# Splitting the first row loads of a top-2 gating kernel further

## The chip, the cores and the metric

The kernel runs on one core of one Trainium2 chip. The metric is device time in microseconds (us), lower is better; the time given is the median of several executions. A profile of one execution is recorded besides; its span (first to last instruction) is a little shorter than the device time.

## The reference

Each of 16 x 1024 tokens has a row `x` of 512 float32 values and 8 router logits. The softmax of the logits gives 8 probabilities; the two largest are kept and scaled to a sum of 1, and the row of `x` is written out twice, once multiplied by each of the two weights, the smaller weight first.

```python
batch, seq, hidden, n_experts, k = 16, 1024, 512, 8, 2

def reference(x, router_logits, k):
    logits_max = np.max(router_logits, axis=-1, keepdims=True)
    probs = np.exp(router_logits - logits_max)
    probs = probs / np.sum(probs, axis=-1, keepdims=True)
    topk_indices = np.argsort(probs, axis=-1)[..., -k:]
    topk_probs = np.take_along_axis(probs, topk_indices, axis=-1)
    topk_probs = topk_probs / np.sum(topk_probs, axis=-1, keepdims=True)
    x_expanded = x[:, :, np.newaxis, :].repeat(k, axis=2)
    return (x_expanded * topk_probs[..., np.newaxis]).astype(np.float32)
```

So 33.5 MB of `x` and 0.5 MB of logits are read from HBM, and 67.1 MB are written to it. There is no matrix product.

## The kernel before

The 16384 tokens are laid over 128 partitions, 128 tokens per partition, in two batches of 65 and 63 tokens per partition. A token's row is 2 KB. All loads of `x` go to one buffer `xs` of 65 tokens per partition, which the second batch fills again. A load of n tokens moves, for each of the 128 partitions, one run of n x 2 KB that is contiguous in HBM: a load of 2 tokens is 128 rows of 4 KB.

```python
GROUPS = [65, 63]

LOADS = [[2, 2, 4, 8, 16, 16, 17], [2, 2, 4, 8, 16, 16, 15]]
...
    L = 16
    ...
    logits = wpool.tile([P, M, E], F32)
    xs = wpool.tile([P, max(GROUPS), D], F32)
    osp = wpool.tile([P, L, 2, D], F32)

    def over(r, n, G):
        a = 2 * r - G
        return xs[:, a : a + 2 * n, :].rearrange("p (r k) d -> p r k d", k=2)

    h = L // 2
    e = 2
    m0 = 0
    for g, G in enumerate(GROUPS):
        r = 0
        for n in LOADS[g]:
            nc.sync.dma_start(xs[:, r : r + n, :], x_v[g][:, r : r + n, :])
            r += n
            if g == 0 and r == L:
                nc.sync.dma_start(logits[:, :G], rl_v[0])
                nc.sync.dma_start(logits[:, G:], rl_v[1])
                WA = top2_weights(nc, wpool, logits, M, E)
        assert r == G
        begin = [(0, e, osp[:, :e]), (e, L - e, osp[:, e:])] if g == 0 else [(0, L, osp)]
        plan = begin + [
            (L, L, over(L, L, 2 * L)),
            (2 * L, h, osp[:, :h]),
            (2 * L + h, h, osp[:, h:]),
        ]
        plan += [(r, n, over(r, n, G)) for r, n in ((48, 8), (56, 4), (60, G - 60))]
        for r, n, og in plan:
            nc.vector.tensor_tensor(
                og,
                xs[:, r : r + n, :].unsqueeze(2).to_broadcast([P, n, 2, D]),
                WA[:, m0 + r : m0 + r + n, :].unsqueeze(3).to_broadcast([P, n, 2, D]),
                op=ALU.mult,
            )

            queue = nc.scalar if n == e else nc.sync
            queue.dma_start(o_v[g][:, r : r + n], og)
        m0 += G
```

The logits of all tokens are loaded once, after the first 16 tokens per partition of `x`. `top2_weights` (lines 13 to 44) finds the two largest logits by 12 VectorE operations in maxima and minima, takes their difference and makes both weights by two sigmoids on ScalarE.

The products (line 125) are made on VectorE, eight of them in the first batch and seven in the second. Their result goes to `osp`, a buffer of 16 tokens, or over rows of `xs` that are no longer needed (`over`). Each is followed by its store (line 133). All loads (line 109) and all stores but one are issued by SyncE, in the order of the program; only the first store, of 2 tokens, is issued by ScalarE. Tile, the layer that the kernel is written in, adds the waits on semaphores: a product waits for its rows and weights, a store for its product, a load of the second batch for the stores that still read the place it fills.

Of the kernel before, what the change touches and what calls it, by code (L numbers as in the profile page):

```python
# [1 line left out]

# [4 lines left out]

F32 = mybir.dt.float32
ALU = mybir.AluOpType
ACTF = mybir.ActivationFunctionType  # L10
P = 128


def top2_weights(nc, pool, logits, M, E):

    hi, lo, n = None, None, E  # L20
    while n > 1:
        n //= 2
        if hi is None:
            a, b = logits[:, :, 0:n], logits[:, :, n : 2 * n]
            nhi = pool.tile([P, M, n], F32, tag=f"hi{n}")
            nlo = b
            nc.vector.tensor_tensor(nhi, a, b, op=ALU.max)  # L27
            nc.vector.tensor_tensor(nlo, a, b, op=ALU.min)  # L28
        else:
            a, b = hi[:, :, 0:n], hi[:, :, n : 2 * n]  # L30
            nhi = pool.tile([P, M, n], F32, tag=f"hi{n}")
            nlo = pool.tile([P, M, n], F32, tag=f"lo{n}")
            tmp = pool.tile([P, M, n], F32, tag=f"tmp{n}")
            nc.vector.tensor_tensor(tmp, lo[:, :, 0:n], lo[:, :, n : 2 * n], op=ALU.max)  # L34
            nc.vector.tensor_tensor(nlo, a, b, op=ALU.min)  # L35
            nc.vector.tensor_tensor(nlo, nlo, tmp, op=ALU.max)  # L36
            nc.vector.tensor_tensor(nhi, a, b, op=ALU.max)  # L37
        hi, lo = nhi, nlo
    dlt = pool.tile([P, M], F32, tag="dlt")
    nc.vector.tensor_tensor(dlt, hi[:, :, 0], lo[:, :, 0], op=ALU.subtract)  # L40
    WA = pool.tile([P, M, 2], F32, tag="WA")
    nc.scalar.activation(WA[:, :, 0], dlt, ACTF.Sigmoid, scale=-1.0)  # L42
    nc.scalar.activation(WA[:, :, 1], dlt, ACTF.Sigmoid, scale=1.0)  # L43
    return WA

GROUPS = [65, 63]

LOADS = [[2, 2, 4, 8, 16, 16, 17], [2, 2, 4, 8, 16, 16, 15]]


@with_exitstack
def kernel(
    ctx: ExitStack,
    tc: tile.TileContext,
    x: bass.AP,
    router_logits: bass.AP,
    k: bass.AP,  # L60
    out: bass.AP,
):
    nc = tc.nc
    B, S, D = x.shape
    E = router_logits.shape[-1]
    N = B * S
    assert int(k) == 2 and E == 8 and N == P * sum(GROUPS)
    M = N // P

    L = 16  # L70
    x_v, o_v, rl_v = [], [], []
    t0 = 0
    for n in GROUPS:
        t1 = t0 + P * n
        x_v.append(
            x.rearrange("b s d -> (b s) d")[t0:t1].rearrange("(p m) d -> p m d", p=P)
        )
        o_v.append(
            out.rearrange("b s k d -> (b s) k d")[t0:t1].rearrange(
                "(p m) k d -> p m k d", p=P  # L80
            )
        )
        rl_v.append(
            router_logits.rearrange("b s e -> (b s) e")[t0:t1].rearrange(
                "(p m) e -> p m e", p=P
            )
        )
        t0 = t1

    wpool = ctx.enter_context(tc.tile_pool(name="wpool", bufs=1))  # L90
# [46 lines that stand above are left out]
# [1 line left out]
_INS = ['x', 'router_logits', 'k']  # L138
_OUTS = [((16, 1024, 2, 512), 'float32')]

_NUMBERS = {'k': 2}


# [26 lines left out]
```

## Time and profile before

| | |
|---|---|
| device time, median of 3 | 240.41 us (240.33 to 240.43) |
| span of the profiled execution | 238.7 us |
| VectorE busy | 142.5 us (60%) |
| ScalarE busy | 1.8 us (1%) |
| DMA packets, bytes | 4464, 101.19 MB |
| first issue of a load on SyncE | 0.73 us |
| logits landed, first VectorE operation | 14.4 us, 14.48 us |
| first product | 18.95 us |
| last product starts, last store issued | 211.65 us, 215.03 us |

How to read it. The profile divides the span into 40 equal slices and gives for each the busy share of an engine in tenths, for the DMA the mean of the core's 16 DMA engines. The list of queues says how much of 16 engines' span the packets of a queue filled. The chain of waits goes back from the last instruction, at each step to what released it. In lists of waits, `SPq` is SyncE's queue, which issues the transfers; an issue is short, and the transfer itself lands later. A DMA packet is here one row of a partition; a DMA ends on each engine with a packet of 4 bytes that signals its completion.

### The profile page before, as it was taken

What the parts mean: (1) busy time and instruction counts of PE and PEld (TensorE: products, weight loads), DVE (VectorE), ACT (ScalarE), POOL (GpSimd) and SP (SyncE); (2) the same over time, 40 slices, a digit from 0 to 9 for tenths busy, and PEclk for the clock granted to TensorE, in tenths of its full rate; (3) what the DMA queues carried; (4) which work ended last, traced back from release to release, by engine and by line L of the source; (5) the groups of instructions that cost most, each with busy time, mean ns of one, the idle gap of its engine ahead of it and who ended that gap; (6) DMA issues with size and microseconds to landing.
All of it is one profiled execution on the core that took longest, in us unless ns stands there. A gap on an engine that the chain in (4) does not pass through costs nothing.

```text
span 238.7 us, 128 instructions
## 1 busy us (share of the span) xinstructions
DVE 142.5 (60%) x26; ACT 1.8 (1%) x3; POOL 0.2 (0%) x4
## 2 busy tenths in 40 slices
DVE  0058999990299699910000699999106999990000
ACT  2000000000000000000000000000000000000000
POOL 0000000000000000000000000000000000000000
DMA  7999998999998999999999999998999989999997
GB/s 253 442 448 439 419 464 375 434 461 461 395 461 351 439 439 439 439 439 406 428 426 439 458 417 412 459 529 373 472 406 406 472 351 439 439 439 439 439 398 305
DMA packets 4464, 101.19 MB, mean 424 GB/s; under 512 B 496, under 2 KB 624, under 8 KB 1264
## 3 DMA queue, kind: packets, MB, share of 16 engines
q1 hardware_dynamic: 4320, 100.14, 97.9%
q10 hardware_dynamic: 144, 1.05, 1.0%
HBM read 34.08 MB, written 67.11 MB: 424 GB/s over the span
## 4 chain that ended last, share of the span: by engine, by line
DMA 41%; DVE 41%; issue 5%; SPq 2%; ACT 0%; DVEq 0%
DVE xs L125 22%; DVE osp L125 17%; DMA out_dram<-osp 13%; DMA out_dram<-xs 12%; DMA xs<-in_x_dram 11%; DMA logits<-in_router_logits_dram 5%; SPq L109 2%; DVE nhi L27 0%; DVE logits L28 0%; SPq L113 0%; DVE nlo L36 0%; DVE nhi L37 0%; DVE nlo L35 0%; DVE tmp L34 0%; SPq L133 0%
## 5 line engine op out<-in xcount | busy, mean ns | idle before, releaser
L125 DVE TENSOR_TENSOR osp<-xs,WA 128x8192 f32<-128x8192 f32 (+3 forms) x7 | 69.1, 9908 | 55.7 <-DMA xs<-in_x_dram 31.3
L125 DVE TENSOR_TENSOR xs<-xs,WA 128x16384 f32<-128x16384 f32 (+4 forms) x8 | 69.5, 8692 | 2.3 <-DMA out_dram<-xs 2.1
L27 DVE TENSOR_TENSOR nhi<-logits 128x512 f32<-128x512 f32 x1 | 0.7, 691 | 14.5 <-DMA logits<-in_router_logits_dram 14.5
L42 ACT ACT_TABLE_LOAD x1 | 1.3, 1283 | 0.7 <-PEq L151 0.7
L28 DVE TENSOR_TENSOR logits<-logits 128x512 f32<-128x512 f32 x1 | 0.7, 691 | 0.0
L37 DVE TENSOR_TENSOR nhi<-nhi 128x256 f32<-128x256 f32 (+1 forms) x2 | 0.7, 352 | 0.0
L35 DVE TENSOR_TENSOR nlo<-nhi 128x256 f32<-128x256 f32 (+1 forms) x2 | 0.7, 352 | 0.0
L36 DVE TENSOR_TENSOR nlo<-nlo,tmp 128x256 f32<-128x256 f32 (+1 forms) x2 | 0.7, 351 | 0.0
L42 ACT ACTIVATE WA<-dlt 128x128 f32<-128x128 f32 x1 | 0.3, 315 | 16.4 <-DVE dlt L40 16.4
L34 DVE TENSOR_TENSOR tmp<-logits 128x256 f32<-128x256 f32 x1 | 0.4, 418 | 0.0
L40 DVE TENSOR_TENSOR dlt<-nhi,nlo 128x128 f32<-128x128 f32 x1 | 0.3, 291 | 0.0
L43 ACT ACTIVATE WA<-dlt 128x128 f32<-128x128 f32 x1 | 0.3, 299 | 0.0
L34 DVE TENSOR_TENSOR tmp<-nlo 128x128 f32<-128x128 f32 x1 | 0.3, 285 | 0.0
L151 POOL MEMSET const-bfloat16-1.0<- 128x1 bf16 x1 | 0.1, 102 | 0.0
L151 POOL MEMSET const-uint8-127<- 128x1 uint8 x1 | 0.1, 102 | 0.0
L151 POOL MEMSET const-float32-1.0<- 128x1 f32 x1 | 0.1, 99 | 0.0
L151 POOL MEMSET const-float32-0.0<- 128x1 f32 x1 | 0.1, 98 | 0.2 <-issue 0.2
## 6 DMA issues: line engine op xcount, KB each, us to landing
xs<-in_x_dram SPq DMA_DIRECT2D x4, 4096.0 KB, 31.2
out_dram<-osp SPq DMA_DIRECT2D x4, 4096.0 KB, 20.7
out_dram<-xs SPq DMA_DIRECT2D x2, 4096.0 KB, 21.2
out_dram<-osp SPq DMA_DIRECT2D x1, 7168.0 KB, 27.7
xs<-in_x_dram SPq DMA_DIRECT2D x1, 4352.0 KB, 41.4
xs<-in_x_dram SPq DMA_DIRECT2D x2, 2048.0 KB, 19.1
out_dram<-xs SPq DMA_DIRECT2D x2, 2048.0 KB, 21.6
xs<-in_x_dram SPq DMA_DIRECT2D x1, 3840.0 KB, 38.2
```

Of the source, the lines that this page charges most:

```text
L27: nc.vector.tensor_tensor(nhi, a, b, op=ALU.max)
L28: nc.vector.tensor_tensor(nlo, a, b, op=ALU.min)
L34: nc.vector.tensor_tensor(tmp, lo[:, :, 0:n], lo[:, :, n : 2 * n], op=ALU.max)
L35: nc.vector.tensor_tensor(nlo, a, b, op=ALU.min)
L36: nc.vector.tensor_tensor(nlo, nlo, tmp, op=ALU.max)
L37: nc.vector.tensor_tensor(nhi, a, b, op=ALU.max)
L40: nc.vector.tensor_tensor(dlt, hi[:, :, 0], lo[:, :, 0], op=ALU.subtract)
L42: nc.scalar.activation(WA[:, :, 0], dlt, ACTF.Sigmoid, scale=-1.0)
L43: nc.scalar.activation(WA[:, :, 1], dlt, ACTF.Sigmoid, scale=1.0)
L109: nc.sync.dma_start(xs[:, r : r + n, :], x_v[g][:, r : r + n, :])
L125: nc.vector.tensor_tensor(og, xs[:, r : r + n, :].unsqueeze(2).to_broadcast([P, n, 2, D]), WA[:, m0 + r : m0 + r + n, :].unsqueeze(3).to_b ...
L151: nc = _bacc.Bacc("TRN2", target_bir_lowering=False, num_devices=1)
```

## The change

The first load of the first batch, of two tokens per partition, is divided into two loads of one token each, and nothing else is touched. The first loads of that batch then have rows of 2, 2, 4, 8 and 16 KB where they had 4, 4, 8 and 16; the second of 4 KB and the later ones stay as they were. The first sixteen tokens are still loaded ahead of the logits. It is meant to bring the first data on the way with smaller pieces and let the queue get going earlier. (The 4 KB rows of the second batch's first two loads are left.)

```diff
-LOADS = [[2, 2, 4, 8, 16, 16, 17], [2, 2, 4, 8, 16, 16, 15]]
+LOADS = [[1, 1, 2, 4, 8, 16, 16, 17], [2, 2, 4, 8, 16, 16, 15]]
```

## The prediction

> **What bounds the kernel now.** I read the page first, then the windows of the start and of the end, then the chain of waits, the waits of the issuing queue, and last the trace's records of single DMA packets. On the page the two rows of slices belong together: the upper is VectorE, the lower the mean busy share of the 16 DMA engines, in tenths.
>
> ```profile
> DVE 142.5 (60%) x26; ACT 1.8 (1%) x3; POOL 0.2 (0%) x4
> DVE  0058999990299699910000699999106999990000
> DMA  7999998999998999999999999998999989999997
> q1 hardware_dynamic: 4320, 100.14, 97.9%
> HBM read 34.08 MB, written 67.11 MB: 424 GB/s over the span
> ```
>
> VectorE is idle for whole slices and the DMA engines never are: only the first and the last slice are below 8. The SyncE queue's packets alone fill 97.9% of 16 engines. The next view gives busy times in stretches; the last two columns are the DMA share (it can pass 1, since a packet is counted where it starts) and GB/s.
>
> ```profile
> 0.00:1.60 1.60, 0.00 (x0) 0.87 (x1) 0.20 (x4) 1.00 0.00 0
> 1.60:2.60 1.00, 0.00 (x0) 0.41 (x1) 0.00 (x0) 1.00 0.80 106
> 2.60:4.80 2.20, 0.00 (x0) 0.00 (x0) 0.00 (x0) 1.00 1.01 395
> 4.80:14.40 9.60, 0.00 (x0) 0.00 (x0) 0.00 (x0) 1.00 1.06 445
> 14.40:60.00 45.60, 38.34 (x14) 0.52 (x2) 0.00 (x0) 1.00 1.02 434
> 180.00:237.00 57.00, 33.77 (x5) 0.00 (x0) 0.00 (x0) 1.00 1.00 432
> 237.00:238.70 1.70, 0.00 (x0) 0.00 (x0) 0.00 (x0) 1.00 0.02 7
> ```
>
> So data moves from about 1.7 us to 237.5, where the last packet ends (it is counted where it started, before 237), without a gap. What isn't full rate is 1.6 us of nothing, one poor microsecond at 106 GB/s, and some 1.2 us after the last byte. The span is therefore: time to the first packet, a loss while the first reads get going, the work of all packets, and the end. Only these four can change it.
>
> The chain of waits names VectorE for 41% of the span, and this must not mislead. Three pieces of it, start and length in us:
>
> ```profile
> 3.25 11.12 DMA logits<-in_router_logits_dram
> 53.53 29.77 DMA out_dram<-xs
> 150.68 30.43 DMA out_dram<-osp
> ```
>
> A store issued at 53.53 lands at 83.30, and one issued at 150.68 at 181.11. A 16-row store is 8 MB, some 19.5 us at 430 GB/s, so each stood about 10 us behind other transfers in the queue. I did this for the other stores as well (issue time from the timeline, landing of the transfer ahead of it from the semaphore events): 36.27 against 47.0, 72.77 against 83.3, 167.94 against 181.1, 198.46 against about 210. **The work waiting ahead of each is about 10 us everywhere**, so VectorE can be late by far more than a microsecond before a DMA engine runs dry.
>
> The first product also waits for the logits (14.5 us in the list of waits), not for the first rows. The issuing queue's own waits on loads are small:
>
> ```profile
> DVE nhi L27 <- DMA logits<-in_router_logits_dram: 14.5, 1, 14.5
> SPq L109 <- DMA xs<-in_x_dram: 1.1, 2, 0.9
> 0.73 1.81 SPq L109 DMA_DIRECT2D xs<-in_x_dram  x4
> 2.58 0.63 SPq L113 DMA_DIRECT2D logits<-in_router_logits_dram  x1
> ```
>
> Four issues in 1.81 us are one every 0.47 us (0.38 to 0.43 us of work and 0.05 between).
>
> **What the Trainium skill says.** All four places are on the page "DMA: Bandwidth & Descriptors".
> - "Latency and other measured facts" gives about 600 ns to the first byte for transfers issued from SyncE. The trace agrees: the first issue ends at 1.11 us and the first packet starts at 1.735, 0.62 us later.
> - "Where 436 GB/s comes from" puts the ceiling of the 16 ports at 435 GB/s, and expects some 358 for traffic with HBM. The trace has 432 to 434 GB/s over long stretches: the 435 holds here, the 358 doesn't.
> - "Why small descriptors are slow (HBM only)" names a fixed cost per packet. The trace agrees, and I take its size from the trace, below.
> - "Rules for kernel authors" asks for at least 1 MiB per DMA. The first loads here are 512 KB, and packets behind them start every 155.5 ns on each engine with no gap, because later DMAs are queued by then; the rule doesn't bite.
>
> **The change part by part.** For the first batch of 65 rows per partition, the first 4 rows come as 1, 1 and 2 in place of 2 and 2. The loads of 4, 8, 16, 16 and 17 rows stay, the logits still follow row 16, and the second batch is untouched. VectorE and ScalarE do the same work.
>
> *Removed:* 128 packets of 4096 bytes (one load of 128 partition rows of 4 KB). *Added:* 256 packets of 2048 bytes (two loads of 2 KB rows) and one more set of 16 completion packets of 4 bytes. Per DMA engine: 8 packets of 4 KB go, 16 of 2 KB and one completion come.
>
> Cost of a packet, from the records of single packets, as the distance between successive starts on one engine while reads alone run:
>
> ```
> bytes    ns from start to start
>  2016     78.7
>  2080     81.3   (the logits)
>  4096    155.5
>  8192    305.9
> ```
>
> From 4096 to 8192 is 150.4 ns for 4096 bytes, 0.0367 ns a byte; 4096 bytes then cost 150.4, and the 5.1 left over is the fixed part. It gives 81.5 for the 2080 bytes of the logits (81.3 seen), so it carries down to this size. 2048 bytes lie between the two logits sizes: 80.0 ns. A completion packet takes 6 ns before the next data packet starts.
> - removed: 8 x 155.5 = 1244 ns
> - added: 16 x 80.0 + 6 = 1286 ns
> - **difference: +42 ns** on every engine, and on the path, since the engines are never idle afterwards.
>
> *The added issue:* 0.47 us on SyncE. Loads and logits behind it are issued 0.47 us later (logits at 3.05 in place of 2.58). This lies beside transfers: with the first sixteen rows issued the queue holds 4 MB in both kernels, over 9 us of work. At the front I checked for a gap: a 2 KB-row load is 0.64 us of transfer, longer than the 0.47 us between issues. The second load's packets can start about 0.62 us after its issue ends at 1.59, so at 2.2; the first is not through before about 3.0. No gap. The two issues that wait for an early load (the second 16-row load, until 4.37, and the 17-row load, until 5.62) may move by up to about 1 us; the queue then has work until about 14 us.
>
> *The start itself:* the first issue stays at 0.73, so the first packet should stay at 1.735. What follows is the one term that I can't work out. Before, the 16 engines finish the first load (8 packets each, 1.24 us at the steady pace) between 3.56 and 4.00 us, 3.80 in the mean, where 1.735 + 1.24 would be 2.98: **a loss of 0.82 us**. The first packet of the engines takes 186 to 993 ns, 588 in the mean. I take this as a latency, paid once whatever the size of the packets: change 0.
>
> Sum: 240.41 + 0.04 + 0 = **240.45 us**.
>
> **The rivals.**
> 1. *The starting loss goes with the bytes of the first packet.* That must be what the change hopes for: first rows half as long, first data half as late. Halving 588 ns saves 0.29 us, and with the 0.04 the time would be 240.16. For it: the first packets are slow, not only late. Against it: several are through in 186 ns with the same 4096 bytes, so bytes don't set their time, and what a first packet saves the next may pay.
> 2. *The starting loss goes with the number of packets.* Up to 2.6 us, 26 packets had started, 1.6 per engine. If so many are slow whatever they carry, the half-size ones bring half the bytes, and 1.6 x (155.5 - 80.0) = 0.12 us are lost: 240.57. For it: starts are sparse up to 2.6 and regular afterwards. Against it: some engines have two or three through by then.
> 3. *VectorE becomes the limit*, since the logits land later. In the ring order their packets stand behind the same 4 MB, so they land about 0.04 us later; even 0.47 us is small against the 10 us of margin. Change 0.
> 4. *A reordered queue.* One more DMA shifts which completion semaphore each later DMA shares with an earlier one. A store that must wait for a transfer still running would cost microseconds. Against it: the sharers are seven or eight transfers back, and the reloads that wait (15.7 us in the waits of the queue) wait for stores that read the same buffer, which stays so. About 1 in 50.
>
> **Range and chances.** The known part is +0.04. Rivals 1 and 2 put the ends at 240.16 and 240.57; three runs of the kernel before spread by 0.10 us, which I add in part on both sides. So 240.2 to 240.7 at 8 in 10. Two per cent would be 4.8 us; the whole start up to 2.6 us is less than that, so a gain of 2% is out of reach, and a loss of 2% needs rival 4. Chances: 0.003 faster, 0.99 same, 0.007 slower.
>
> **What would show it.** In the profile after: 4608 packets in place of 4464 (128 data and 16 completions more), five loads in the first group of issues, first packet near 1.7 us, logits issued near 3.05 and landed near 14.4, VectorE's first work near 14.5, the last packet's end near 237.5. If the window from 1.6 to 2.6 us moves clearly more than 106 GB/s and the logits land near 14.1, rival 1 is right; if they land at 14.5 or later, rival 2. A dip of the DMA slices in mid-span would be rival 4, and would make the prediction wrong.

## The result and the profile after

The changed kernel takes **242.55 us** (242.34 to 243.09, 4 runs) against 240.42 for the kernel before: ratio 1.0091, 95% interval 1.0074 to 1.0109. The prediction said 240.45, at most 240.7. The change costs 2.1 us, fifty times the 0.04 us that the packets were to cost. (The profiled execution, from which the traces below come, is the longest of the four, 243.09 us; that of the kernel before took 240.51.)

The page of the changed kernel, the lines that answer to those of before:

```profile
DVE 142.5 (59%) x26; ACT 1.8 (1%) x3; POOL 0.2 (0%) x4
DVE  0018999992099889920000599999105999990000
DMA  6999999999999999999999999999999999999994
DMA packets 4608, 101.19 MB, mean 419 GB/s; under 512 B 512, under 2 KB 640, under 8 KB 1408
q1 hardware_dynamic: 4464, 100.14, 97.0%
```

The work is the same to the packet: 4608 packets, as foreseen, and the same 142.5 us of VectorE. The mean rate fell from 424 to 419 GB/s. The row of slices hides where, for it is a mean over 16 engines in slices of 6 us. The windows of the same profile show it (the last two columns are DMA share and GB/s):

```profile
1.60:2.60 1.00, 0.00 (x0) 0.41 (x1) 0.00 (x0) 1.00 0.62 172
2.60:4.80 2.20, 0.00 (x0) 0.00 (x0) 0.00 (x0) 1.00 0.92 290
4.80:14.40 9.60, 0.00 (x0) 0.00 (x0) 0.00 (x0) 1.00 0.97 374
14.40:30.00 15.60, 12.38 (x13) 0.51 (x2) 0.00 (x0) 1.00 1.04 445
237.00:238.00 1.00, 0.00 (x0) 0.00 (x0) 0.00 (x0) 1.00 0.67 283
238.00:239.00 1.00, 0.00 (x0) 0.00 (x0) 0.00 (x0) 1.00 0.20 86
239.00:240.00 1.00, 0.00 (x0) 0.00 (x0) 0.00 (x0) 1.00 0.12 49
```

The start is better than before (172 in place of 106 GB/s), and then it turns: 290 where 395 stood, 374 where 445 stood. Note also the share beside the rate: 0.97 busy at 374 GB/s means packets that are counted as running and wait. Others are not even running: by the packet records, 12.8 packets are under way at once from 3.5 to 4.8 us, where the kernel before has 16.4, so three or four of the 16 engines stand without one. From 14.4 us on the rate is as before. The last three lines are the bill: at 237 us the kernel before had next to nothing left to move (7 GB/s from there to its end), and here the rate falls from 283 to 49 GB/s over three more microseconds, as one engine after the other is done.

The chain of waits has the logits landing 2.5 us later (3.53 + 13.34 = 16.87 in place of 14.38), and the timeline of SyncE's queue has what I had not foreseen, issues that take long:

```profile
3.53 13.34 DMA logits<-in_router_logits_dram
0.73 2.28 SPq L109 DMA_DIRECT2D xs<-in_x_dram  x5
3.06 0.43 SPq L113 DMA_DIRECT2D logits<-in_router_logits_dram  x1
3.53 1.11 SPq L114 DMA_DIRECT2D logits<-in_router_logits_dram  x1
4.68 3.60 SPq L109 DMA_DIRECT2D xs<-in_x_dram  x3
```

The second issue of logits takes 1.11 us, where it took 0.44, and the first of the three loads behind it 1.36.

The trace has sixteen semaphore events for each DMA, one from each DMA engine, so it gives a landing per engine. First and last of the 16, in us:

```
                       before             after
first load             3.91 to 4.37       2.83 to 3.44
second load            5.17 to 5.62       3.62 to 4.07
third load             7.65 to 8.11       5.10 to 7.93
logits, second half   13.91 to 14.38     14.81 to 16.87
last store           237.31 to 237.85    237.65 to 240.50
```

(The third load is the one of 4 tokens before and of 2 after.) The engines of the kernel before stay about half a microsecond apart in these rows. In the changed kernel they part during the third load, and the distance is not made up in the remaining 230 us: the first engine ends 0.3 us later than before, the last 2.65. A load has 128 packets and 16 completion events, so 8 packets to an engine, and a late engine is not seen to get help. The waits don't end with the third load either: of the 128 packets of the 4-token load behind it, which start between 4.8 and 9.8 us, 48 take longer than the 309 ns of the kernel before, up to 1600.

### The profile page after: what moved, and what is told of

Read it like the earlier page. It is cut to its first block, busy times and chain, and to the rows that moved or that the text cites. A ratio compares the mean times of both kernels' runs of the same rounds, so it can differ in the third digit from the quotient of the medians.

```text
span 241.3 us, 131 instructions
## 1 busy us (share of the span) xinstructions
DVE 142.5 (59%) x26; ACT 1.8 (1%) x3; POOL 0.2 (0%) x4
## 2 busy tenths in 40 slices
DMA packets 4608, 101.19 MB, mean 419 GB/s; under 512 B 512, under 2 KB 640, under 8 KB 1408
## 4 chain that ended last, share of the span: by engine, by line
DMA 42%; DVE 40%; issue 5%; SPq 2%; ACT 0%; DVEq 0%
DVE xs L125 22%; DVE osp L125 17%; DMA out_dram<-osp 13%; DMA out_dram<-xs 12%; DMA xs<-in_x_dram 12%; DMA logits<-in_router_logits_dram 6%; SPq L109 2%; DVE nhi L27 0%; DVE logits L28 0%; DVE nlo L36 0%; DVE nhi L37 0%; DVE nlo L35 0%; DVE tmp L34 0%; SPq L113 0%; SPq L133 0%
```

## The experiments

All change only how the first batch is loaded. "Time" is the median; "logits" is the landing of the second half of the logits, first and last engine, in the one execution that was profiled. The ratio is to the kernel before on the same chip.

```
first batch                     time us   ratio (95% interval)      logits
before  2 2 4 8 16 16 17        240.42                              13.91 to 14.38
after   1 1 2 4 8 16 16 17      242.55    1.0091 (1.0074, 1.0109)   14.81 to 16.87
set 1   1 3 4 8 16 16 17        240.58    0.9979 (0.9957, 1.0000)   13.74 to 14.82
        2 1 1 4 8 16 16 17      240.97    1.0007 (0.9995, 1.0019)   14.69 to 15.24
        2 2 4 8 8 8 16 17       240.57    0.9996 (0.9977, 1.0015)   13.87 to 14.25
        1 1 6 8 16 16 17        243.10    1.0092 (1.0060, 1.0124)   14.12 to 17.36
set 2   8 1 1 6 16 16 17        240.62    0.9978 (0.9957, 0.9998)   13.91 to 14.41
        1 1 1 1 4 8 16 16 17    242.42    1.0060 (1.0037, 1.0082)   14.17 to 15.82
        2 in two halves, 2 4 .. 243.03    1.0082 (1.0051, 1.0113)   15.08 to 16.96
        1 15 16 16 17           240.77    0.9985 (0.9963, 1.0007)   13.68 to 14.39
set 3   16 16 16 17             240.86    1.0012 (1.0005, 1.0019)   13.68 to 14.62
        1 x8, 8 16 16 17        241.72    1.0048 (1.0034, 1.0061)   14.74 to 15.65
        4 1 1 10 16 16 17       240.59    1.0001 (0.9992, 1.0009)   13.89 to 14.63
        after, 2nd on ScalarE   240.57    1.0000 (0.9992, 1.0009)   13.94 to 14.55
```

(In sets 1 and 2, 22 of 68 executions of the kernel before took 241.7 to 242.6 us, and so did 4 of 20 of the kernel 2 2 4 8 8 8; none of these was profiled and the reason stays open, and as they shift the ratios of these sets a little, the medians are the better guide.)

The last engine's landing of the logits and the time of the same execution go together: in twelve of the fourteen rows they lie 225.6 to 226.5 us apart, 226.1 before and 226.2 after the change. So what the change costs has happened to the slowest engine by the time the logits land. The two other rows are 1 3 4 (227.1) and 16 16 16 17 (227.4). Their profiled executions took 241.93 and 242.03 us, the longest of 12 and of 22, and one engine fell back further after the logits; they don't speak for the medians.

**Set 1: is it the rows or the number of DMAs?** The changed kernel has both 2 KB rows and one DMA more.

```diff
-LOADS = [[2, 2, 4, 8, 16, 16, 17], ...
+LOADS = [[1, 3, 4, 8, 16, 16, 17], ...
```

> First batch loaded as 1, 3, 4, 8, 16, 16, 17: one 2 KB-row load in front, no added DMA. Rows theory (2 KB rows in front make the engines stall once the 4 KB and 8 KB rows follow, each engine keeps its own delay to the end): some of the 2.1 us, 241.0 to 242.5. Count theory (one DMA more in the first issues backs up SyncE's descriptor work, seen as issues of 1.1 and 1.4 us in place of 0.43, and starves engines): as before, 240.3 to 240.6. Chance theory (every kernel with another start draws other stalls): anywhere from 239.8 to 243.

Measured: 240.58, not to be told from the kernel before. The range of the rows theory (241.0 and more) is missed. In the profiled execution, the longest, fifteen engines stay together (they land the 4-token load between 7.48 and 7.82 us) and one is 0.76 us behind them (8.58).

```diff
+LOADS = [[2, 1, 1, 4, 8, 16, 16, 17], ...
```

> First batch loaded as 2, 1, 1, 4, 8, 16, 16, 17: as many DMAs and 2 KB rows as the change has, but the 4 KB-row load stays first. Rows theory, where only the first packets matter: about 240.45 (0.04 us of packet cost). Count theory: 242 to 243, with issues of the logits or of the load after them over 1 us. Chance theory: 239.8 to 243.

Measured: 240.97, issues of 0.43 us. Between the theories: a small loss, most of it not at the 2 KB rows but behind them. The first sixteen packets of the 4-row load that follows show it, in ns, in order of start; the same load in the kernel before beside it:

```
2 1 1 4:  1267 1413 531 519 1446 1342 1088 994 1126 618 928 319 319 613 309 309
before:    309  309 309 309  309  309  309 309  309 309 309 309 309 309 309 309
```

Most engines wait at the start of the next load, by different times; later packets of that load average 14 ns more than 309.

```diff
+LOADS = [[2, 2, 4, 8, 8, 8, 16, 17], ...
```

> First batch loaded as 2, 2, 4, 8, 8, 8, 16, 17: one DMA more, none of 2 KB rows, and the added one stands after the logits, when 4 MB are queued. Rows theory: 240.4 to 240.6. Count theory: slower by 1 to 2.5 us if it is the number of descriptors in the queue that matters, as before if it is their number before the logits. Spread of the 16 engines at the landing of the logits: 0.5 us by the rows theory, over 1.5 us by the count theory.

Measured: 240.57 in the median, spread of the engines 0.4 us. One DMA more behind the logits costs nothing.

```diff
+LOADS = [[1, 1, 6, 8, 16, 16, 17], ...
```

> First batch loaded as 1, 1, 6, 8, 16, 16, 17: the change's two 2 KB-row loads with no added DMA. Rows theory: about as the changed kernel, 242 to 243. Count theory: 240.3 to 240.6. Chance theory: 239.8 to 243.

Measured: 243.10 without any added DMA, and the long issue is back at the same place: the seventh issue, here the first of the 16-row loads, takes 1.38 us of the 3.12 below. The timeline of SyncE's queue and two windows of this kernel:

```profile
3.04 0.43 SPq L114 DMA_DIRECT2D logits<-in_router_logits_dram  x1
3.51 3.12 SPq L109 DMA_DIRECT2D xs<-in_x_dram  x3
```

```profile
2.60:3.50 0.90, 0.00 (x0) 0.00 (x0) 0.00 (x0) 1.00 0.98 366
3.50:4.80 1.30, 0.00 (x0) 0.00 (x0) 0.00 (x0) 1.00 0.96 358
4.80:8.00 3.20, 0.00 (x0) 0.00 (x0) 0.00 (x0) 1.00 1.00 370
```

The kernel before in the last two of these windows:

```profile
3.50:4.80 1.30, 0.00 (x0) 0.00 (x0) 0.00 (x0) 1.00 1.02 419
4.80:8.00 3.20, 0.00 (x0) 0.00 (x0) 0.00 (x0) 1.00 1.08 458
```

The count theory falls; two 2 KB-row loads in front are enough. The chance theory is weakened, not gone: the four executions here lie between 242.97 and 243.38, the twelve of 2 1 1 4 between 240.49 and 241.23, but the kernel before varies by 2 us with one and the same start. Between 3.5 and 4.0 us only 12 packets of the 6-row load start, so some of the 16 engines stand without any packet at all. That pointed to descriptors: the Trainium skill's page "DMA: Bandwidth & Descriptors", section "SWDGE vs HWDGE vs iDMA", says that for transfers of SyncE and ScalarE a piece of hardware writes the descriptors that the engines work from. (The trace doesn't record descriptors; it only shows packets that start late or run long.) A load is issued every 0.47 us, and two 2 KB-row loads are eaten in 0.64 us each. If the descriptors of the third load aren't there when an engine gets to it, it waits.

**Set 2: give the descriptors a lead, or take it away.**

```diff
+LOADS = [[8, 1, 1, 6, 16, 16, 17], ...
```

> First batch loaded as 8, 1, 1, 6, 16, 16, 17: the two 2 KB-row loads stay, with a load of 5 us in front of them. Descriptor theory (the generator of descriptors needs about 1 us per DMA while data flows; engines eat a 2 KB-row load in 0.65 us, catch up with it and wait at the first packet of the next load, each by its own time): the lead is large, so no waits, 240.3 to 240.7, with the engines' landings of the logits within 0.6 us. Memory theory (2 KB rows 130 KB apart upset the reads that follow them): waits right behind the two small loads as in the changed kernel, 241.5 to 243.

Measured: 240.62, spread 0.5 us. The same two small loads and again a 6-row load behind them, and all of its packets take exactly 460 ns. So 2 KB rows do not upset what follows them here. The windows of this kernel, and then those of the changed one:

```profile
1.60:2.60 1.00, 0.00 (x0) 0.41 (x1) 0.00 (x0) 1.00 1.12 262
2.60:3.50 0.90, 0.00 (x0) 0.00 (x0) 0.00 (x0) 1.00 0.78 328
3.50:4.80 1.30, 0.00 (x0) 0.00 (x0) 0.00 (x0) 1.00 1.04 429
4.80:8.00 3.20, 0.00 (x0) 0.00 (x0) 0.00 (x0) 1.00 0.95 394
8.00:14.40 6.40, 0.00 (x0) 0.00 (x0) 0.00 (x0) 1.00 1.08 448
```

```profile
3.50:4.80 1.30, 0.00 (x0) 0.00 (x0) 0.00 (x0) 1.00 0.85 243
4.80:8.00 3.20, 0.00 (x0) 0.00 (x0) 0.00 (x0) 1.00 0.95 307
8.00:14.40 6.40, 0.00 (x0) 0.00 (x0) 0.00 (x0) 1.00 0.98 408
```

Length times rate, summed over the five windows, is what had been started by 14.4 us: 0.262 + 0.295 + 0.558 + 1.261 + 2.867 = 5.24 MB here, the same 5.24 MB in the kernel before, and 4.41 MB in the changed one (0.172 + 0.324 in its first two). The missing 0.84 MB are 1.9 us at 430 GB/s. (Packets count whole where they start, so this is rough: by the landings of the logits the mean engine is 1.46 us later than before, 15.62 against 14.16, and the last 2.49.)

```diff
+LOADS = [[1, 1, 1, 1, 4, 8, 16, 16, 17], ...
```

> First batch loaded as 1, 1, 1, 1, 4, 8, 16, 16, 17: four 2 KB-row loads in front. Descriptor theory: the engines outrun the generator for twice as long, at least the changed kernel's loss: 242.5 to 245, waits already within the third and fourth load (from 3.5 us on). Memory theory: waits only when larger rows follow, so from about 4.9 us on, 242 to 243.

Measured: 242.42, just below the range of the descriptor theory and inside that of the memory theory. But the waits begin within the third small load: it lands between 4.41 and 5.78 us over the engines, after 3.58 to 4.00 for the second. They need no larger rows, which speaks against the memory theory.

```diff
-nc.sync.dma_start(xs[:, r : r + n, :], x_v[g][:, r : r + n, :])
+cuts = [(0, 64), (64, P)] if g == 0 and r == 0 else [(0, P)]
+for a, b in cuts:
+    nc.sync.dma_start(xs[a:b, r : r + n, :], x_v[g][a:b, r : r + n, :])
```

> The first load of 2 tokens (4 KB rows) issued as two DMAs of 64 partitions each: as many DMAs and bytes per DMA as the change has in front, rows of 4 KB, half as many descriptors per DMA. Descriptor theory with a cost per DMA: as the changed kernel, 242 to 243; with a cost per descriptor: 240.3 to 240.7. Memory theory (row size): 240.3 to 240.7.

Measured: 243.03, but this settles nothing. The two halves bring costs of their own: issues of 0.55 to 0.58 us, a first packet at 2.05 in place of 1.735, and 4 KB packets of 260 to 309 ns in place of 159 for most of the time from 3.6 to 4.9 us. On top come three engines that land the next load over a microsecond after the others (7.57 to 7.82, the rest by 6.56). Whether the cost is per DMA or per descriptor stays open.

```diff
+LOADS = [[1, 15, 16, 16, 17], ...
```

> First batch loaded as 1, 15, 16, 16, 17: one 2 KB-row load to start on, then one with 9 us of work. Descriptor theory: no engine ever catches up, and the quicker start seen with a 2 KB-row load in front (0.2 in place of 0.5 us of waiting per engine up to 2.6 us) stays: 239.9 to 240.3. Memory theory: 240.3 to 241, with some waits in the second load.

Measured: 240.77. Hardly any waits after the first 3.5 us (the longest 0.25 us), but no gain either. The first engine does land the logits 0.23 us earlier than before (13.68), the last one doesn't (14.39). A quicker start for the average engine is worth nothing if the slowest has none.

**Set 3: how much lead, one stumble or many, and a second queue.**

```diff
+LOADS = [[16, 16, 16, 17], ...
```

> First batch loaded as 16, 16, 16, 17: three DMAs and 24 data packets per engine fewer ahead of the logits, the most lead that the descriptors can have. Descriptor theory: no waits after the first 3 us, all 16 engines land the logits within 0.6 us of each other; 3 x (8 x 5.1 + 6) ns = 0.14 us less packet cost, so 240.2 to 240.6, and no slower execution among the repeats. If large first rows hurt the start (the first data of the engines come later): 240.6 to 241.5.

Measured: 240.86, slower than before by 0.12% (0.05 to 0.19). This is the second expectation: large first rows did hurt the start a little. In the profiled execution the first load lands over 0.96 us (12.34 to 13.30), from waits in the engines' first packets, which all start by 2.2 us. What else that execution lost, it lost later (last section).

```diff
+LOADS = [[1, 1, 1, 1, 1, 1, 1, 1, 8, 16, 16, 17], ...
```

> First batch loaded as eight times 1, then 8, 16, 16, 17. If the supply of descriptors is too slow per DMA throughout, the loss grows with the number of small loads: 8 x (1.0 - 0.65) = about 3 us or more, 243.5 to 246. If the engines stumble once, when the first few descriptors are used up, and are then supplied in time: as the four small loads, 242 to 243.

Measured: 241.72, below both ranges and less than with two. The last engine's landings of the eight loads are 3.45, 4.05, 6.18, 6.82, 7.47, 8.12, 8.79 and 9.40: one stumble of about 1.5 us at the third, then 0.61 to 0.67 us each, full speed. The first engine needs 0.68 to 0.88 us for each from the third on. So no lasting shortage; those in front are held up a little at each load, and the late ones come nearer.

```diff
+LOADS = [[4, 1, 1, 10, 16, 16, 17], ...
```

> First batch loaded as 4, 1, 1, 10, 16, 16, 17: the two 2 KB-row loads behind 2.5 us of lead, half of what the 8-row load gave. Descriptor theory: nearly no waits, 240.3 to 241.0. Memory theory (already weak after the 8-row load): 241.5 to 243.

Measured: 240.59. A load of 2.5 us in front is lead enough. With the 2-token load in front (2, 1, 1, 4; 1.24 us of work) 0.3 us were lost against the 240.65 of its set, with nothing in front 2.1.

```diff
+first = nc.scalar if g == 0 and r == 1 else nc.sync
-nc.sync.dma_start(xs[:, r : r + n, :], x_v[g][:, r : r + n, :])
+first.dma_start(xs[:, r : r + n, :], x_v[g][:, r : r + n, :])
```

> The changed kernel (1, 1, 2, 4, 8, 16, 16, 17) with its second 2 KB-row load issued by ScalarE. If the supply is limited for SyncE's queue alone, the engines have descriptors from a second ring and SyncE's third load is issued 0.47 us earlier: most of the loss goes, 240.4 to 241.3. If the supply is limited for all queues together: as the changed kernel, 242 to 243.

Measured: **240.57**, as the kernel before (240.54 in this set), with all of the changed kernel's loads and packets. The timelines of ScalarE's and of SyncE's queue, then the windows of this kernel:

```profile
0.73 0.41 ACTq L110 DMA_DIRECT2D xs<-in_x_dram  x1
```

```profile
0.73 1.80 SPq L110 DMA_DIRECT2D xs<-in_x_dram  x4
3.18 0.45 SPq L115 DMA_DIRECT2D logits<-in_router_logits_dram  x1
```

```profile
1.60:2.60 1.00, 0.00 (x0) 0.85 (x1) 0.00 (x0) 1.00 0.71 111
3.50:4.80 1.30, 0.00 (x0) 0.00 (x0) 0.00 (x0) 1.00 1.07 425
4.80:8.00 3.20, 0.00 (x0) 0.00 (x0) 0.00 (x0) 1.00 1.07 453
```

Both small loads are issued at 0.73, the third at 1.16 in place of 1.64, so that it has 0.47 us more of lead. The dent of 243 GB/s from 3.5 to 4.8 us is gone. The Trainium skill (same page, "Issuing engines are not separate DMA queues") says that issuing from several engines saves only the issuer's time, usually little. The issue time saved is indeed 0.47 us; here the kernel takes 2 us less. Whether the earlier third load did it or the second queue itself, this run doesn't separate, and the changed kernel was not run again beside it.

## Why the prediction was wrong

- **The bound and the margin** were right. VectorE started 2.5 us later and no store came near the end of its queue: the first large one was issued at 38.77, and the transfer ahead of it landed on the first engine at 46.96.
- **The packet cost** was right: successive starts of 2048-byte packets are 80 ns apart, and the counts of packets are those foreseen.
- **"No gap" at the front is the step that failed.** I took a load's packets to be able to start 0.62 us after its issue ends, as seen for the first load, compared single loads with the issue interval (0.64 against 0.47 us), and looked for a gap ahead of the second load only. By that reckoning the third load, issued by 2.06, was ready at 2.7 and needed at 3.56, when its first packet started. The engines waited for it nevertheless: it lands between 5.10 and 7.93 us, and 12.8 packets are under way from 3.5 to 4.8 us in place of 16.4. The runs show when this happens: with two small loads in front, not with the same two behind 2.5 or 5 us of work, nor with one of them on the other queue.
- **The added issue "beside transfers"**: the first six issues took 0.38 to 0.43 us, but the seventh took 1.11 and the eighth 1.36, which I had not foreseen. They are a sign, not shown to be a cost: the load of the eighth issue was out at 6.04, and the logits ahead of it land from 14.81 on.
- **A second step failed silently: I treated 16 engines as one.** The logits land 1.46 us later on the mean engine and 2.49 on the last, and the last one sets the end: the last store lands 2.65 us later on it, 1.08 in the mean (238.61 against 237.53).
- **The starting loss** did shrink, as rival 1 had it and I did not. The first load landed at 3.19 in the mean in place of 4.16; 0.60 of the difference is its smaller size, the rest, about 0.35, is gain. That overstates it, for two other kernels with the same 4 KB rows in front lose less at the start than the kernel before (last section). It was given back behind the second load.
- **Rivals 2, 3 and 4** were not what happened. Waiting for data that is already queued was not among my rivals.

Shown is that engines wait at the loads behind the small ones, that some stand without a packet, and that a longer load ahead, or the second small load on another queue, removes the loss. That descriptors are what is missing is inferred: a packet that runs long doesn't show what it waits for. No kernel here contradicts it, but the times expected from it were missed with 1 1 1 1, eight times 1 and 1 15. A longer load ahead also moves the small loads to a later time; that it isn't the time alone is shown by the two-queue run only, which has them at the same time as the changed kernel. Where in the supply the time is lost, whether per DMA or per descriptor, why one engine loses little and another 2 us, and whether the long executions of the kernel before have the same cause, stays open.

## What to carry to other kernels

At the start of a kernel, while the queue is still being filled, don't put two small loads (here 256 KB each) at the head of one queue: begin with a load that lasts 2.5 us, or issue the second small one from another queue; both were tried on this kernel alone. A DMA-bound kernel ends with its slowest DMA engine, so look at the landings engine by engine, and at whether the DMA rate falls off in steps at the end of the span; a mean of 9 tenths in every slice can hide 2 us. Making the first load smaller gained nothing in any of these kernels; the first computation waits for another transfer here, the logits.

## What the runs showed of the hardware

- The delay of an engine in the first 8 us was still there 230 us later (2.06 us between first and last engine at the logits, 2.85 at the end, so it even grew).
- A single engine can fall behind later too, with no small load near: in the profiled execution of 16 16 16 17 one engine lands the third 16-token load 0.54 us after the other fifteen (36.40 against 35.86 at most), the 17-token load 1.45 us after them (48.32 against 46.87), and the last store still 1.46 us after them (239.18 against 237.72).
- A first load with 2 KB rows loses 0.48 us in the mean in the changed kernel (its completion packets at 2.85 us less 1.73 less 0.64), and 0.41 to 0.51 in the five others that begin with one on SyncE alone. One with 4 KB rows loses 0.82 in the kernel before, but 0.56 and 0.58 in 2 1 1 4 and 2 2 4 8 8 8.
- A DMA over 64 partitions took longer to issue than one over 128 (0.55 to 0.58 against 0.43 us), and from 3.6 to 4.9 us most of the 4 KB packets took 260 to 309 ns in place of 159.
